# A decoder block in eight-row column tiles: the next block's norm applied 3, 3, 2 instead of 2, 3, 3

## The chip, the cores and the metric

The kernel runs on one core of a Trainium2 chip. The metric is the device time of one execution in microseconds (us). Three executions of the kernel before took 1915.47, 1916.68 and 1917.81 us; the median is 1916.68 us.

## The reference, cut to what matters

One layer, sequence 2048, model width 1024, all float32:

```
h    = rmsnorm(x, norm1)                      # over the 1024 channels
proj = h @ w_in                               # q, k, v, B, C, hc, p: 1792 columns
attn, conv, pool = three mixers on proj       # window-128 attention, conv of 3, trailing means
x    = x + concat(attn, conv, pool) @ w_out   # the output projection
x    = x + relu(rmsnorm(x, norm2) @ w1)^2 @ w2
out  = rmsnorm(x, final_norm)
```

The change concerns the first line of it alone: when the normed rows `h` of the next block of tokens are made.

## The kernel before, in words

Activations are kept transposed: channels on the 128 partitions, tokens on the free axis. The 1024 channels are KC = 8 row tiles, and the sequence is NB = 4 blocks of T = 512 tokens. For each block b the kernel runs the input projection (14 column tiles, from L874 on; each is 8 row tiles times 3 matmuls), the mixers beside it, and then the output projection `out_proj(b, c)` (L736), 8 column tiles c of 24 matmuls each. After the last block come the two MLP matrix products in a Strassen-like form, which the change does not touch.

Every float32 matrix product is made of three matmuls on split operands, high and low part (`mm3`, L284 to L287): high by high (L285), high weight by low data (L286), low weight by high data (L287). So each row tile of the normed input has a high part `xh` and a low part `xl`, and the projection reads the row tiles in the order k = 0 to 7.

`norm_apply(b, k)` (L402) makes one such row tile for a block after the first, with three instructions: VectorE (DVE) multiplies the raw row tile `xr` by the norm's weight and by the broadcast row of reciprocal norms `rb` (`hf`, L417); ScalarE (ACT) casts that to the high part (`xh`, L418); VectorE subtracts (`xl`, L419). These run while TensorE works on the output projection of the block before: the loop over its column tiles (L926 to L930) gives column tiles 0 and 1 the squares, 2 the reciprocal root, 3 the row's store, 4 the row's broadcast load (`rb`, L362), and 5, 6 and 7 the eight applications. `out_proj(b, c)` then adds the residual on VectorE (`xo`, L745), stores it, squares it on ScalarE (`sr`, L752) and adds the square on GpSimd (POOL, `acc`, L753). `hf`, `sr` and others share one pool of four buffers (tag `tmp`).

The weights stream by themselves: SyncE's queue (SP) loads a raw tile `wr` (L208), ScalarE casts the high part `wh` (L263), GpSimd subtracts the low part `wl` (L264).

The order of the instructions on each engine is not the program's text. A planner simulates the engines and gives each free engine the ready instruction that is earliest in the program; the engines then run these orders as they are, and wait where the chip is later than the plan. So an instruction from later in the program can stand ahead of an earlier one. Two such matter here. On ScalarE the first square of the block after next (`acc<-xr`, L383, from `norm_square`) stands among the casts of `norm_apply`: it reads a raw tile that can be loaded only when `norm_apply` has freed the buffer (tag `xr`, 8 buffers). And in the last block the raw buffers go, one by one, to `first_blocks` (L818, called with k = 0 to 3), which loads parts of the residual for the MLP (`xb`, L824), scales them on VectorE (L830) and subtracts them from each other (L784): the scales of the parts with an odd number use a row that is there early (`rb_acc`), the others one that takes the buffer of `rb` and so is loaded (`rb_rb`, L362) after the last `hf` of the block.

Of the kernel before, what the change touches and what calls it, by code (L numbers as in the profile page):

```python
# [84 lines left out]
def tile_trunk(  # L85
# [226 lines left out]
    def tmp(name):  # L312
        return pB.tile([P, T], F32, tag="tmp", name=name, bufs=4)
# [61 lines left out]
    def norm_load(b, k):  # L375
        t = pA.tile([P, T], F32, tag="xr", name=f"xr{b}_{k}", bufs=KC)
        sp.dma_start(t, xT[k * P : (k + 1) * P, b * T : (b + 1) * T])
        xr[b, k] = t
# [12 lines left out]
    def norm_rstd(b):  # L391
        nr[b] = cst.tile([P, 4], F32, tag="nr", name=f"r1_{b}", bufs=2)
        rstd_of(nacc[b], nr[b], starts(T), ps_tr, "tr", f"n1_{b}")

    def norm_bcast(b):
        rbs[b] = pB.tile([P, T], F32, tag="rb", name=f"rb{b}")
        if b == 0:
            act.copy(rbs[b], bcast(nr[b], T, ps_tr, "tr", f"n1_{b}"))
        else:
            row_load(rbs[b], "n1", b * T)  # L400
# [32 lines left out]
    def build_bias():  # L433

        for h in range(NH):
            ps = ps_tr.tile([P, T], F32, tag="tr", name=f"pse{h}")
            pe.matmul(ps[:, :ELEN], rl[:, h : h + 1].to_broadcast([P, P]), oh, start=True, stop=True)

            e = tmp(f"e{h}")[:, :ELEN]
            act.activation(e, ps[:, :ELEN], AF.Copy, scale=math.sqrt(HD))  # L440
            sp.dma_start(esc[h], e)

    def skew_bias():
        full = esc[:]
        skew = bass.AP(full.tensor, full.offset + P - 1, [[ELEN - 1, P], [P * ELEN, NH], [1, 2 * P]])
        sp.dma_start(bias, skew)
# [28 lines left out]
    def load_pw():  # L475
        for g in range(4):
            o = (g % 2) * 64
            sp.dma_start(pwr[o : o + 64, g // 2, o : o + 64], pw[g])
# [3 lines left out]
    def load_rows():  # L482
        for i in range(2):
            for a in range(2):
                rowt[i, a] = pA.tile([P, T], F32, tag="xr", name=f"wr{i}_{a}", bufs=KC)
                sp.dma_start(
                    rowt[i, a].rearrange("p (c n) -> p c n", n=P),
                    wout.rearrange("c p r -> p c r")[:, a * HC : (a + 1) * HC, i * P : (i + 1) * P],
                )

    def build_rows():

        for i in range(2):
            act.activation(pwr[:, i], pwr[:, i], AF.Copy, scale=prm[:, PPS + i : PPS + i + 1])
            t = pA.tile([P, 2 * T], F32, tag="s", name=f"wx{i}", bufs=2)
            for a in range(2):
                ps = ps_tr.tile([P, T], F32, tag="tr", name=f"pwx{i}_{a}")
                pe.matmul(ps, pwr[:, i], rowt[i, a], start=True, stop=True)
                act.copy(t[:, a * T : (a + 1) * T], ps)
            late.append(  # L500
                lambda i=i, t=t: sp.dma_start(wx[:, :, i * P : (i + 1) * P], t.rearrange("p (c n) -> p c n", n=P))
            )
# [16 lines left out]
    def start_first(tiles):  # L519

        ws = [(w_next(0), w_next(0)) for _ in tiles]
        xh, xl = xhl[0]
        pss = [ps_mm.tile([P, T], F32, tag="mm", name=f"pj0_{i}") for i in tiles]
        for step in range(KC + 2 * len(tiles) - 2):
            for n, (w, ps) in enumerate(zip(ws, pss)):
                k = step - 2 * n
                if 0 <= k < KC:
                    hi, lo = w[k // HC]
                    mm3(ps, hi[:, k % HC], lo[:, k % HC], xh[:, k], xl[:, k], k == 0, k == KC - 1)
        first.update(zip(tiles, pss))  # L530

    def proj(b, i, mid=None, bank=None):
        if b == 0 and i in first:
            ps = first[i]
            flush()
        else:
            xh, xl = xhl[b]
            ps = ps_mm.tile([P, T], F32, tag="mm", name=f"pj{b}_{i}") if bank is None else bank
            for k in range(KC):
                if k % HC == 0:  # L540
                    hi, lo = w_next()
                if k == HC and mid:
                    mid()
                latest[0] = mm3(ps, hi[:, k % HC], lo[:, k % HC], xh[:, k], xl[:, k], k == 0, k == KC - 1)
        return ps

    def scaled(b, i, ps):
        if b:
            return ps
        z = pB.tile([P, T], F32, tag="xo", name=f"z{i}", bufs=2)  # L550
        dve.tensor_tensor(out=z, in0=ps, in1=rbs[0], op=ALU.mult)
        return z
# [208 lines left out]
    def norm2_rstd(b, psp, tag):  # L761
        rstd_of(acc2[b], rstd2[:, 4 * b : 4 * b + 4], starts(T), psp, tag, f"n2_{b}")

    def norm2_row(b, psp, tag, t):
        row_store(rstd2[:, 4 * b : 4 * b + 4], "n2", b * T, T, psp, tag, f"n2_{b}", t)
# [96 lines left out]
    for b in range(NB):  # L862
        if b == 0:
            start_first(IN_ORDER[:3])
            load_pw()
            norm_rstd(0)
            build_bias()
            bank = ps_sc.tile([P, 2, T], F32, tag="sc", name="pj0_q")
            first[IN_ORDER[3]] = proj(0, IN_ORDER[3], bank=bank[:, 0])
            norm_bcast(0)  # L870
            skew_bias()
            load_rows()
        for i in IN_ORDER[:NPRE]:
            ps = proj(b, i)  # L874
            evac[i](b, scaled(b, i, ps))
        if b:
            norm2_rstd(b - 1, ps_tr, "tr")
        else:
            build_rows()
        st1, st2 = {}, {}  # L880
        for n, i in enumerate(IN_ORDER[NPRE:]):
            if n < KC and b + 1 < NB:
                norm_load(b + 1, n)

            def mid(n=n):
                if 2 <= n < 10:
                    st2[n] = att_trans(*st1.pop(n - 2))

            ps = proj(b, i, mid)
            if b and n == 1:  # L890
                norm2_row(b - 1, ps_tr, "tr", tmp(f"row2_{b}"))
            if 2 <= n < 10:
                av = att_av(*st2.pop(n))
            evac[i](b, scaled(b, i, ps))
            if 2 <= n < 10:
                att_out(*av, dve if n > 5 else gp)
            if n < 8:
                st1[n] = att_scores(b, *units[n])
            if n == 5:
                do_pool(b, 0)  # L900
            elif n == 7:
                do_pool(b, 1)
            if 2 <= n < 4 and b + 1 < NB:
                norm_square(b + 1, n - 2, gp)
            if b + 1 == NB:
                with tc.issue_after(latest[0].ins):
                    if n == 0:
                        first_rows()
                    for k, at in enumerate(FIRST):
                        for step in range(3):  # L910
                            if n == at[step]:
                                first_blocks(k, step)
        if b + 1 == NB:
            sA.close()
            pH, sH = opened("pH", bufs=1, side="right")
            pX, sX = opened("pX", bufs=1, side="right")
        for c in range(KC):
            if b + 1 < NB:
                if c < 2:
                    for k in range(2 + c * 6 // 2, 2 + (c + 1) * 6 // 2):  # L920
                        norm_square(b + 1, k, dve)
                elif c == 2:
                    norm_rstd(b + 1)
                elif c == 3:
                    row_store(nr[b + 1], "n1", (b + 1) * T, T, ps_tr, "tr", f"n1_{b + 1}", tmp(f"row1_{b}"))
                elif c == 4:  # L926
                    norm_bcast(b + 1)
                else:
                    for k in {5: (0, 1), 6: (2, 3, 4), 7: (5, 6, 7)}[c]:
                        norm_apply(b + 1, k)  # L930
            else:
                per = NEARLY * HC / KC
                if c == 0:
                    for i in range(int(per)):
                        first_load(i)
                for i in range(int(per * c), int(per * (c + 1))):
                    first_take(i)
                for i in range(int(per * (c + 1)), int(per * (c + 2))):
                    if i < NEARLY * HC:
                        first_load(i)  # L940
            out_proj(b, c)
# [400 lines left out]
```

## Time and profile before

| what | value |
|---|---|
| median of three executions | 1916.68 us |
| the profiled execution's own time | 1912.7 us |
| its span on the core | 1910.9 us |
| TensorE (PE) busy | 1875.3 us, 98% of the span |
| VectorE busy | 1114.4 us, 58% |
| ScalarE busy | 894.2 us, 47% |
| GpSimd busy | 1020.9 us, 53% |

The profile is of one execution. The span is what the core's instructions cover, and the profiled execution's time is 1.8 us more. Engines run beside each other; an engine's idle time costs something only where TensorE, which is busy nearly all of the span, has to wait because of it. Below, a row of a timeline gives the start and the length in us, the engine, the line, the operation, what it writes and reads, a count of merged instructions, and in brackets the idle time before it and what ended that. "Boundary" is the passage from one block's output projection to the next block's input projection; there are three.

### The profile page before, as it was taken

To read this page: it belongs to the slowest core of one execution; us is meant where nothing else is said; L and a number is where in the kernel's file an instruction comes from. 1 tells how busy PE (TensorE), PEld (TensorE's weight loads), DVE (VectorE), ACT (ScalarE), POOL (GpSimd) and SP (SyncE) were. 2 spreads that over 40 slices of the span, in tenths; PEclk is the share of its full clock that TensorE was granted. 3 is DMA by queue.
4 is the path that set the end of the run, shared out by engine and by line. 5 is a ranking of instruction groups with operands and counts; after the bars stand their busy time and mean duration, and the time that the engine had idled before them with its cause. 6 is when DMAs were issued, how large, how long until landed. Compare 5 with 4: busy or idle time off the path is not lost.

```text
span 1910.9 us, 25904 instructions
## 1 busy us (share of the span) xinstructions
PE 1875.3 (98%) x8507; PEld 1527.7 (80%) x8507; DVE 1114.4 (58%) x1606; ACT 894.2 (47%) x1637; POOL 1020.9 (53%) x745
## 2 busy tenths in 40 slices
PE   8989999999899999999999999999999999999998
PEld 6867887888787888888878888888888888888887
DVE  5695585576888577865574444442525264533465
ACT  6654664663476444554565455442323222225332
POOL 5667566575563645654464444434666665526520
PEclk9999999999999999999999999999999999999999
DMA  8417426425936779765686656588777666645244
GB/s 261 139 61 219 123 67 208 129 72 183 313 105 217 241 252 316 274 219 195 226 282 202 198 178 194 187 276 281 238 236 237 196 214 203 221 131 166 99 160 138
DMA packets 202938, 375.46 MB, mean 196 GB/s; under 512 B 22775, under 2 KB 43316, under 8 KB 202804
## 3 DMA queue, kind: packets, MB, share of 16 engines
q1 hardware_dynamic: 201992, 373.20, 60.3%
q8 instruction: 67, 1.10, 0.2%
q10 hardware_dynamic: 812, 0.61, 0.1%
q14 instruction: 67, 0.55, 0.1%
HBM read 249.45 MB, written 117.98 MB: 192 GB/s over the span
## 4 chain that ended last, share of the span: by engine, by line
PE 84%; DMA 6%; DVE 6%; issue 2%; ACT 1%; POOL 1%; SPq 1%; DVEq 0%; POOLq 0%; ACTq 0%
PE o L285 11%; PE o L286 11%; PE o L287 11%; PE bT L287 6%; PE bT L286 6%; PE bT L285 6%; PE bB L285 4%; PE bB L286 4%; PE bB L287 4%; PE pj L286 4%; PE pj L285 4%; PE pj L287 4%; PE po L286 1%; PE po L285 1%; PE po L287 1%
## 5 line engine op out<-in xcount | busy, mean ns | idle before, releaser
L264 POOL TENSOR_TENSOR wl<-wr,wh 128x512 fp32r<-128x512 f32 x354 | 502.9, 1427 | 516.0 <-ACT wh L263 477.8
L263 ACT CAST wh<-wr 128x512 fp32r<-128x512 f32 x416 | 254.5, 617 | 345.5 <-PE bT L286 62.6
L784 DVE TENSOR_TENSOR bl<-br,bh 128x1024 fp32r<-128x1024 f32 (+2 forms) x144 | 186.9, 1301 | 320.9 <-ACT bh L1131 318.0
L286 PE MATMUL o<-bl,wh 128*128 128x512 f32 (+1 forms) x960 | 362.0, 380 | 0.0
L287 PE MATMUL o<-bh,wl 128*128 128x512 f32 (+1 forms) x960 | 361.2, 380 | 0.0
L285 PE MATMUL o<-bh,wh 128*128 128x512 f32 (+1 forms) x960 | 349.7, 380 | 0.0
L286 PEld LDWEIGHTS o<-bl,wh 128*128 128x128 f32 x960 | 180.9, 188 | 36.6 <-DVE bl L784 0.2
L287 PEld LDWEIGHTS o<-bh,wl 128*128 128x128 f32 x960 | 180.8, 188 | 36.7
L285 PEld LDWEIGHTS o<-bh,wh 128*128 128x128 f32 x960 | 176.4, 188 | 36.4
L286 PE MATMUL bT<-hlT,wh 128*128 128x512 f32 x512 | 202.2, 395 | 1.0 <-POOL hlT L987 1.0
L287 PE MATMUL bT<-hhT,wl 128*128 128x512 f32 x512 | 202.0, 395 | 0.0
L285 PE MATMUL bT<-hhT,wh 128*128 128x512 f32 x512 | 201.8, 394 | 0.0
L285 PE MATMUL pj<-xh,wh 128*128 128x512 f32 x440 | 177.7, 405 | 7.0 <-ACT wh L263 6.5
L286 PE MATMUL pj<-xl,wh 128*128 128x512 f32 x440 | 176.2, 401 | 4.1 <-DVE xl L419 4.1
L287 PE MATMUL pj<-xh,wl 128*128 128x512 f32 x440 | 176.3, 401 | 0.0
L264 POOL TENSOR_TENSOR wl<-s,wh 128x512 fp32r<-128x512 f32 x64 | 92.2, 1440 | 137.7 <-ACT wh L263 128.9
L263 ACT CAST wh<-s 128x512 fp32r<-128x512 f32 x64 | 39.7, 621 | 247.4 <-PE o L286 238.8
L1131 ACT CAST bh<-br 128x1024 fp32r<-128x1024 f32 (+2 forms) x144 | 123.2, 856 | 64.4 <-PE o L287 55.5
L285 PE MATMUL bB<-hhB,wh 128*128 128x512 f32 x384 | 151.7, 395 | 0.0
L286 PE MATMUL bB<-hlB,wh 128*128 128x512 f32 x384 | 151.4, 394 | 0.0
L287 PE MATMUL bB<-hhB,wl 128*128 128x512 f32 x384 | 151.3, 394 | 0.0
L231 POOL TENSOR_TENSOR s<-wr,wr 128x512 f32<-128x512 f32 x64 | 127.9, 1999 | 15.3 <-DMA wr<-in_w_dram 10.6
(186 smaller groups left out, 3368.5 us busy)
## 6 DMA issues: line engine op xcount, KB each, us to landing
wr<-in_w_dram SPq DMA_DIRECT2D x256, 256.0 KB, 3.6
hop_T<-s SPq DMA_DIRECT2D x128, 256.0 KB, 2.9
wr<-in_win_dram SPq DMA_DIRECT2D x112, 256.0 KB, 4.3
hop_B<-h SPq DMA_DIRECT2D x96, 256.0 KB, 3.3
br<-hop_B SPq DMA_DIRECT2D x48, 512.0 KB, 4.5
br<-hop_T SPq DMA_DIRECT2D x48, 512.0 KB, 4.5
wr<-ss_T SPq DMA_DIRECT2D x48, 256.0 KB, 2.9
wr<-in_wout_dram SPq DMA_DIRECT2D x36, 256.0 KB, 2.6
```

What stands on the lines that cost most here:

```text
L231: gp.tensor_tensor(out=t, in0=a, in1=b, op=op)
L263: act.copy(hi, src)
L264: eng.tensor_tensor(out=lo, in0=src, in1=f32(hi), op=ALU.subtract)
L285: pe.matmul(ps, hi, xh, start=first, stop=False)
L286: pe.matmul(ps, hi, xl, start=False, stop=False)
L287: return pe.matmul(ps, lo, xh, start=False, stop=last)
L784: return dve.tensor_tensor(out=out, in0=a, in1=b, op=ALU.subtract)
L1131: mark["act"] = act.copy(hi, src)
```

## The change

In the loop over the output projection's column tiles, the eight applications of the next block's norm are dealt out differently: column tile 5 gets row tiles 0, 1 and 2 instead of 0 and 1, column tile 6 gets 3, 4 and 5 instead of 2, 3 and 4, and column tile 7 gets 6 and 7 instead of 5, 6 and 7. Nothing else is edited.

```
@@ -926,7 +926,7 @@
                 elif c == 4:
                     norm_bcast(b + 1)
                 else:
-                    for k in {5: (0, 1), 6: (2, 3, 4), 7: (5, 6, 7)}[c]:
+                    for k in {5: (0, 1, 2), 6: (3, 4, 5), 7: (6, 7)}[c]:
                         norm_apply(b + 1, k)
             else:
                 per = NEARLY * HC / KC
```

## Rows read from the trace of the kernel before

**Rows 1.** Waits of TensorE over the whole span: total us, times, longest us.

```profile
PE pj L286 <- DVE xl L419: 4.1, 4, 2.9
...
PE sc L610 <- DMA q<-ql: 3.4, 5, 1.5
```

**Rows 2.** Timeline of TensorE at the first boundary.

```profile
182.51 0.39 PE L285 MATMUL pj<-xh,wh 128*128 128x512 f32 x1
...
183.81 0.39 PE L285 MATMUL pj<-xh,wh 128*128 128x512 f32 x1
```

**Rows 3.** Timeline of TensorE at the second boundary.

```profile
329.46 0.39 PE L285 MATMUL pj<-xh,wh 128*128 128x512 f32 x1
...
332.94 0.40 PE L285 MATMUL pj<-xh,wh 128*128 128x512 f32 x1
```

**Rows 4.** Timeline of TensorE at the third boundary, into the last block.

```profile
474.54 0.40 PE L285 MATMUL pj<-xh,wh 128*128 128x512 f32 x1
...
477.81 0.39 PE L287 MATMUL pj<-xh,wl 128*128 128x512 f32 x1
478.73 0.50 PE L285 MATMUL pj<-xh,wh 128*128 128x512 f32 x1 [0.53 <-ACT xh L418]
482.10 0.80 PE L286 MATMUL pj<-xl,wh 128*128 128x512 f32 x1 [2.87 <-DVE xl L419]
...
488.63 0.40 PE L285 MATMUL pj<-xh,wh 128*128 128x512 f32 x1
```

**Rows 5.** One stretch there: busy us by engine, granted TensorE clock, DMA share, GB/s.

```profile
484.00:486.00 2.00, 2.00 (x5) 1.59 (x6) 2.00 (x4) 0.32 (x1) 0.00 (x0) 0.50 0.89 289
```

**Rows 6.** Timeline of VectorE at the second boundary, column tiles 5 to 7.

```profile
313.84 1.35 DVE L419 TENSOR_TENSOR xl<-hf,xh 128x512 fp32r<-128x512 f32 x2
316.93 0.69 DVE L745 TENSOR_TENSOR xo<-po,xo 128x512 f32<-128x512 f32 x1 [1.74 <-DMA xo<-in_xT_dram]
...
325.25 0.68 DVE L745 TENSOR_TENSOR xo<-po,xo 128x512 f32<-128x512 f32 x1
325.85 3.55 DVE L417 SCALAR_TENSOR_TENSOR hf<-xr,prm,rb 128x512 f32<-128x512 f32 x3
329.33 2.98 DVE L419 TENSOR_TENSOR xl<-hf,xh 128x512 fp32r<-128x512 f32 x3
```

**Rows 7.** Timeline of ScalarE in the same stretch.

```profile
318.85 0.63 ACT L383 ACTIVATE acc<-xr 128x512 f32<-128x512 f32 x1 [3.86 <-DMA xr<-in_xT_dram]
```

**Rows 8.** Timeline of VectorE at the third boundary.

```profile
461.84 1.46 DVE L419 TENSOR_TENSOR xl<-hf,xh 128x512 fp32r<-128x512 f32 x2
467.69 0.75 DVE L830 SCALAR_TENSOR_TENSOR xb<-xb,prm,rb_acc 128x512 f32<-128x512 f32 x1 [4.40 <-DMA xb<-x1s]
468.36 0.69 DVE L745 TENSOR_TENSOR xo<-po,xo 128x512 f32<-128x512 f32 x1
...
477.28 3.08 DVE L417 SCALAR_TENSOR_TENSOR hf<-xr,prm,rb 128x512 f32<-128x512 f32 x3
480.29 4.03 DVE L419 TENSOR_TENSOR xl<-hf,xh 128x512 fp32r<-128x512 f32 x3
...
485.50 4.80 DVE L830 SCALAR_TENSOR_TENSOR xb<-xb,prm,rb_rb 128x512 f32<-128x512 f32 x4
```

**Rows 9.** The instructions of tile hf: ns min/median/max, first and last start, forms.

```profile
L417 DVE SCALAR_TENSOR_TENSOR hf<-xr,prm,rb x24: 737/745/1793, 163.1 to 478.6; 128x512 f32<-128x512 f32 x24
...
L419 DVE TENSOR_TENSOR xl<-hf,xh x24: 676/770/1791, 165.2 to 483.6; 128x512 fp32r<-128x512 f32 x24
```

**Rows 10.** Timeline of the SyncE queue at the third boundary.

```profile
480.39 0.32 SPq L362 DMA_DIRECT2D rb_rb<-row_n  x1
```

**Rows 11.** Timelines of VectorE and TensorE in the last block's input projection.

```profile
499.78 0.68 DVE L594 TENSOR_TENSOR ql<-pj,q 64x512 fp32r<-64x512 f32 x1
...
509.27 0.36 PE L610 MATMUL sc<-Kd,q 128*128 128x256 f32 x1 [1.55 <-DMA q<-ql]
509.59 0.39 PE L285 MATMUL pj<-xh,wh 128*128 128x512 f32 x1
```

More of the change, by code (lines that the diff above doesn't have):

```diff
@@ L928, in tile_trunk @@
                 else:
-                    for k in {5: (0, 1), 6: (2, 3, 4), 7: (5, 6, 7)}[c]:
+                    for k in {5: (0, 1, 2), 6: (3, 4, 5), 7: (6, 7)}[c]:
                         norm_apply(b + 1, k)
```

## The prediction

> **What bounds the kernel now.** I read first the waits of TensorE, then its timeline at the three boundaries, then the timelines of the engines that make it wait there. TensorE is the bound nearly everywhere, so only what makes it wait counts. Among its waits the reader is to see that matmuls on the low part of the normed input (`xl`) waited 4 times, 4.1 us in all and 2.9 at the longest [rows 1]. All four lie at the three boundaries, where the next block's input projection begins and the last applications of the norm are not done.
>
> The wait alone is not the price. At full clock one matmul follows another every 0.234 us: 15 matmuls of row tiles 0 to 4 start from 474.54 to 477.81, 14 steps [rows 4]. First boundary: three steps from 182.51 to 183.81 took 1.30 us in place of 0.70, so 0.60 is lost [rows 2]. Second: nine steps from 329.46 to 332.94 took 3.48 in place of 2.10, 1.38 lost [rows 3]. Third: sixteen steps from 477.81 to 488.63 took 10.82 in place of 3.74, 7.08 lost [rows 4]. There TensorE stood still for 0.53 and 2.87 us and then had a granted clock of 0.50, the 1.2 GHz level [rows 5]: the 14 steps from 482.10 to 488.63 took 6.53 in place of 3.27, so 3.26 of the loss is the clock. All three boundaries together hold 9.06 us, 0.5% of the time; that is the most this change can fetch where it acts.
>
> Why VectorE is late: in column tiles 6 and 7 it has six instructions of `norm_apply` and one residual add. At the second boundary the last six run from 325.85 to 332.31, 6.46 us or 1.08 each [rows 6]; at the third from 477.28 to 484.32, 7.04 or 1.17 each [rows 8]. Seven of these are more than TensorE's 24 x 0.234 = 5.6 us for a column tile. In column tile 5 it has four, and then stands idle: 1.74 us before `xo` at 316.93, which waited for its own load [rows 6], and 4.40 us before 467.69, where a scale of `first_blocks`, planned ahead of `xo`, waited for a transfer [rows 8].
>
> **The change part by part.** It adds, removes and resizes no instruction. Six groups of three (`hf`, `xh`, `xl`) move: row tiles 2 and 5 at three boundaries, each one column tile earlier. No DMA is issued by them; but the buffer that `hf` reads comes free earlier, so one load of a raw tile (or of `xb`) on SyncE's queue may go earlier. That I cost at nothing: these loads are wanted a block later, and the queue's other loads have five weight tiles of lead over TensorE. If the cover is gone, it is a load ahead of the weights on that queue, 0.3 to 0.4 us of issue (0.32 for one such [rows 10]).
>
> Column tile 5: `hf` and `xl` of row tile 2 on VectorE cost from 0.737 + 0.676 = 1.41 to 1.793 + 1.791 = 3.58 us [rows 9]; by the mean of 1.08, 2.16. The idle 1.74 takes nearly all of it [rows 6]; 0.4 is left over, and `xo` comes that much later. Queued behind `xo` are its store, its square and the next group's `hf`. The next group's first `xl` stood idle anyway for a cast behind the square at 318.85, which itself waited 3.86 us for a load [rows 7], so the 0.4 is swallowed there. I take nothing for it; its bounds are 0 and 3.58 - 1.74 = 1.84.
>
> Column tile 6 has as many instructions as before, others by number. I leave `xo` at 325.25 [rows 6].
>
> Column tile 7 has four in place of six. Second boundary: 325.85 + 4 x 1.08 = 330.2 for the last `xl` instead of 332.31. TensorE wants it seven steps after 329.46, at 331.1. The loss of 1.38 goes, with 0.9 to spare. First boundary: the last `xl` was late by 0.60 and comes 2.16 earlier. The loss goes. Together 1.98 us, from 0.60 (the second stays) to 1.98.
>
> Third boundary: in column tile 5 the scale at 467.69 still waits for its transfer, which began when the second `hf` freed a buffer, and that is not moved. The new pair fits into the 4.40 us of standing idle, and `xo` stays at 468.36 [rows 8]. Column tile 7 then runs from 477.28 to 477.28 + 4 x 1.17 = 482.0 in place of 484.3: VectorE is 2.34 us ahead. TensorE wants row tile 6 at 474.54 + 19 x 0.234 = 479.0 and 7 at 479.7, gets them at 480.8 and 482.0, and so still loses about 2.3, and up to 3.3 more if its clock falls again. It gains between 1.5 and 4.8 there.
>
> What is late next: in the last block VectorE's queue is full behind this. It goes straight on to the scales at 485.50 [rows 8] and, with the subtractions and evacuations between, to `ql` at 499.78; the first score matmul at 509.27 waits 1.55 us for the DMA of that `ql` [rows 11]. So whatever TensorE gains beyond VectorE's 2.34 it gives back at that wait. I take 2.2 for the third boundary, between 0 (the transfers of `first_blocks` hold the chain) and 7.08.
>
> Sum: 1.98 + 2.2 = 4.2 us. Against the profiled execution's own time, 1912.7 us (1910.9 of span and 1.8 around it), that is 1908.5. This execution is 4.0 below the median of the runs shown, 1916.68, from which the same 4.2 gives **1912.5 us**.
>
> One rule speaks against this sum. The row first: the 24 `hf` have a median of 745 ns and a maximum of 1793 [rows 9], so an instruction is either plain or held up. The Trainium skill (SBUF — State Buffer, SBUF: two separate sides) says that VectorE with two SBUF inputs and GpSimd reading SBUF share a port pair by an exclusive lock, held for a whole instruction. The trace agrees in the two kinds of duration. By that rule the delay belongs to GpSimd's instructions, whose number does not change, and a pair taken out saves only its plain time.
>
> **The rivals.**
> The pair is cheap: GpSimd's work delays what is left in column tile 7 as often as before, and the pair saves 1.41 instead of 2.34 at the third boundary. The second still fits (332.31 - 1.41 = 330.9 against 331.1). Gain 1.98 + 1.4 = 3.4, 1913.3 us. For it: the two kinds of duration [rows 9]. Against: six instructions and three of GpSimd don't meet in a fixed way.
>
> The last block is held by its transfers: the row for the later scales (`rb_rb`) is loaded at 480.39, after the last `hf` [rows 10], and the queue, stores and loads behind it may not come earlier when VectorE does. Then the third boundary's gain ends as a longer wait at 509.27, and 1.98 is left: 1914.7 us. For it: the DMA share of 0.89 [rows 5]. Against: the load is issued as soon as `hf` has gone, and that is earlier.
>
> The planner puts `xo` ahead of the scale, since VectorE comes free later in its plan too. Then the rest of the idle, 4.40 - 2.34, and the scale itself (468.36 - 467.69) leave the path as well: 2.34 + 2.06 + 0.67 = 5.1, in all 7.1, 1909.6 us. Against: the scale was planned before `xo` with 4.4 us of room on the chip, and 1.4 to 2.3 of it are used.
>
> Slower: at the first two boundaries the cast of row tile 2 is planned behind the square that waits until 318.85 [rows 7]. Now that `xl` of row tile 2 stands ahead of `xo`, `xo` waits too: square done at 319.5, cast and subtraction 1.3 more, `xo` at 320.8, six instructions of 1.08 from 321.5 to 328.0, four more after the next `xo` from 328.7 to 333.0, against 331.1 wanted. The loss at the second boundary becomes 1.9 + 0.1, that of the first grows alike, 0.6 each, so the 1.98 turns into -1.2, and the third leaves +2.2. What decides is the clock: it stayed up after a stall of 1.55 (the next matmul took 0.39 [rows 11]) and fell after 0.53 and 2.87 [rows 4, 5]. One fall costs 3.26: -2.2 + 1.2 + 3.3 = +2.3, 1919.0 us; without it 1915.7. For it: the square does stand among these casts. Against: it needs a transfer that begins when the first `hf` is done, and the new cast needs only the third.
>
> **How the numbers follow.** My forecast has 0.42, the cheap pair 0.13, held by transfers 0.18, `xo` ahead 0.14, slower 0.13. The likeliest is 1912.5, by itself 1911.0 to 1914.0. The range of 1909.0 to 1918.0 takes in nearly all but the fall of the clock and the far half of `xo` ahead. About 0.2%, 3.8 us, is what a measurement of this kernel can tell from no change; the forecast lies just past it. Faster by more: some two thirds of the forecast, `xo` ahead, a little of the cheap pair, 0.45. Within: the rest of these, held by transfers, and the slower case without a fall, 0.45. Slower by more: 0.10.
>
> **What would show it.** After the change TensorE should have no wait for `xl` at the first two boundaries; at the third the last `xl` should end near 482.0 less the 2 us gained before, `xo` of column tile 5 should still stand behind the waiting scale, and the wait of the scores for `ql` should be longer than 1.55. I am wrong if the first two waits stay, if the square stands ahead of the third cast, if VectorE is no earlier after the third boundary, or if TensorE's waits are gone and the time is the same.

## The result and the profile after

The changed kernel takes 1919.04 us (median of 20 runs, 1913.21 to 1923.42), the kernel before 1915.03 (20 runs, 1911.16 to 1917.81): a ratio of 1.0021, 95% interval 1.0013 to 1.0029. It is slower by about 4 us; 4.2 faster was forecast. The profiled execution has a span of 1913.5 us and an own time of 1915.3, so it is one of the quicker ones. Executions of one kernel lie up to 12 us apart (1908.1 to 1920.4 in one kernel below), so below the ratios decide, and a trace only shows where its own execution went.

The waits of TensorE over the whole span, after (total us, times, longest):

```profile
PE sc L610 <- DMA q<-ql: 6.6, 6, 4.1
...
PE pj L286 <- DVE xl L419: 3.3, 2, 2.6
...
PE sc L610 <- ACT vt L575: 1.2, 1, 1.2
```

Against [rows 1] the waits for `xl` fall from 4.1 to 3.3 us, and both that are left are at the third boundary. The waits of the scores for the query copies (`q<-ql`) double, from 3.4 to 6.6, and one for `vt` is new. TensorE's timeline at the second boundary, which shows no wait for `xl` any more, and behind it the first score matmuls (`sc`) of the block that begins there. That is block 2, counted from 0; the expectations below call it block 1:

```profile
350.94 0.36 PE L610 MATMUL sc<-Kd,q 128*128 128x256 f32 x1 [1.24 <-ACT vt L575]
...
352.47 0.36 PE L610 MATMUL sc<-Kd,q 128*128 128x256 f32 x1 [1.05 <-DMA q<-ql]
...
353.40 0.63 PE L287 MATMUL pj<-xh,wl 128*128 128x512 f32 x1
```

The profile puts the first wait down to `vt`, a copy on ScalarE that ended at 350.78. But the scores do not need it: before, the first of them ran ahead of that copy. Before, TensorE and ScalarE:

```profile
350.35 0.28 PE L610 MATMUL sc<-Kd,q 128*128 128x256 f32 x1
```

```profile
351.00 0.59 ACT L575 COPY vt<-pj 128x512 f32<-128x512 f32 x1
```

The first query copy, issued at 343.62, took 7.2 us to land, until 350.85, so the first wait too is one for the copies. Windows over the same place (us, busy us by engine, granted clock, DMA share, GB/s):

```profile
352.00:354.00 2.00, 1.53 (x6) 0.94 (x6) 0.00 (x0) 0.00 (x0) 0.00 (x0) 0.76 1.04 271
354.00:356.00 2.00, 2.00 (x7) 1.71 (x7) 0.00 (x0) 0.00 (x0) 0.00 (x0) 0.50 0.80 206
```

Behind the two waits the clock is at the 1.2 GHz level for a while (0.50). From the first matmul of the input projection to the first transpose of the softmax (`pt`, L638), the stretch in which all this lies, the second boundary took 36.50 us before and takes 39.32 after, although the 1.38 of [rows 3] is gone. The first took 36.29 and takes 36.37: most of its 0.60 of [rows 2] went into waits for `q` (0.4 before, 0.6 after) and for a weight cast (0.3).

Why are the copies late? They are issued on SyncE's queue, which starts its DMAs one after the other and waits at the head for what the next one needs. The queue before, at the second boundary (start, us, operation):

```profile
324.35 0.33 SPq L743 DMA_DIRECT2D xo<-in_xT_dram  x1
324.77 0.38 SPq L377 DMA_DIRECT2D xr<-in_xT_dram  x1
...
325.96 0.33 SPq L746 DMA_DIRECT2D x1s<-xo  x1
327.06 0.33 SPq L377 DMA_DIRECT2D xr<-in_xT_dram  x1
...
330.52 0.33 SPq L743 DMA_DIRECT2D xo<-in_xT_dram  x1
...
337.11 0.33 SPq L743 DMA_DIRECT2D xo<-in_xT_dram  x1
...
338.00 0.63 SPq L566 DMA_DIRECT2D Kd<-Kd  x1
...
340.83 0.99 SPq L598 DMA_DIRECT2D q<-ql  x1
```

and after:

```profile
326.56 0.33 SPq L743 DMA_DIRECT2D xo<-in_xT_dram  x1
326.98 0.38 SPq L377 DMA_DIRECT2D xr<-in_xT_dram  x1
327.45 0.38 SPq L208 DMA_DIRECT2D wr<-in_win_dram  x1
327.93 0.38 SPq L746 DMA_DIRECT2D x1s<-xo  x1
328.36 0.86 SPq L377 DMA_DIRECT2D xr<-in_xT_dram  x1
...
334.46 0.33 SPq L743 DMA_DIRECT2D xo<-in_xT_dram  x1
...
339.98 0.33 SPq L743 DMA_DIRECT2D xo<-in_xT_dram  x1
...
340.87 0.63 SPq L566 DMA_DIRECT2D Kd<-Kd  x1
...
343.62 0.49 SPq L598 DMA_DIRECT2D q<-ql  x1
```

The loads of the raw tiles (`xr`) of the block after next, whose buffers come free earlier, have moved up by one: between the residual load and the store of column tile 6 (`x1s`) stood the fifth of them before (324.77) and stands the sixth after (326.98), and three in place of two are ahead of the store of column tile 5. The store of column tile 6 is issued 1.97 us later (TensorE itself is 0.39 later). The load of a residual tile (`xo`, two buffers) waits for that store: it is issued 4.56 us behind it before, 6.53 after, with three raw loads in between before and two after. The next `xo` load waits in the same way for the store of column tile 7, and right behind it come the key copies: they start 12.0 us after the projection before, 14.5 after, and the first query copy slips by 2.8 (0.39 of it TensorE's).

The two loads that hold the queue there are not urgent themselves. They are the 17th and 18th of the 32 `xo` loads, eight to a block, so they are for column tiles 0 and 1 of block 2; VectorE's add that reads the first of them runs at 439.06 before, 108 us after its issue. To hold these two behind the copies was not tried.

VectorE there, after, in column tiles 5 to 7:

```profile
317.68 0.69 DVE L745 TENSOR_TENSOR xo<-po,xo 128x512 f32<-128x512 f32 x1 [0.71 <-DMA xo<-in_xT_dram]
...
326.22 0.68 DVE L745 TENSOR_TENSOR xo<-po,xo 128x512 f32<-128x512 f32 x1
...
329.63 1.46 DVE L419 TENSOR_TENSOR xl<-hf,xh 128x512 fp32r<-128x512 f32 x2
```

Against [rows 6] the work of the norm ends earlier, at 331.09 for the last `xl` in place of 332.31, but the residual add of column tile 6 comes 0.97 later.

The third boundary. VectorE, after:

```profile
470.49 0.75 DVE L830 SCALAR_TENSOR_TENSOR xb<-xb,prm,rb_acc 128x512 f32<-128x512 f32 x1 [1.82 <-DMA xb<-x1s]
471.16 0.68 DVE L745 TENSOR_TENSOR xo<-po,xo 128x512 f32<-128x512 f32 x1
...
480.07 1.40 DVE L417 SCALAR_TENSOR_TENSOR hf<-xr,prm,rb 128x512 f32<-128x512 f32 x2
481.40 1.78 DVE L830 SCALAR_TENSOR_TENSOR xb<-xb,prm,rb_acc 128x512 f32<-128x512 f32 x1
483.10 3.44 DVE L419 TENSOR_TENSOR xl<-hf,xh 128x512 fp32r<-128x512 f32 x2
```

The idle time before the waiting scale shrinks from 4.40 [rows 8] to 1.82, as forecast. But in column tile 7 a scale of 1.78 us has come ahead of the last two `xl`. The last one ends 8.8 us after TensorE started this projection, against 9.8 before: 1.0 earlier, not the 2.34 of the prediction. TensorE there, after:

```profile
484.90 0.50 PE L286 MATMUL pj<-xl,wh 128*128 128x512 f32 x1 [2.59 <-DVE xl L419]
...
486.59 0.80 PE L286 MATMUL pj<-xl,wh 128*128 128x512 f32 x1 [0.73 <-DVE xl L419]
...
512.02 0.55 PE L610 MATMUL sc<-Kd,q 128*128 128x256 f32 x1 [4.09 <-DMA q<-ql]
```

The eleven steps from 481.92 to 489.68 took 7.76 us in place of 2.57: the loss is 5.19, where it was 7.08 [rows 4]. The 1.9 us gained, and more, come back as the wait of 4.09, where it was 1.55 [rows 11]: the first score matmul runs 34.3 us after the projection's start, against 34.7 before. The clock behind it is at 0.50, where it had stayed at 1.00.

### The profile page after: what moved, and what is told of

Its sections match the earlier page's. It is cut to its first block, busy times and chain, and to the rows that moved or that the text cites. A ratio compares the mean times of both kernels' runs of the same rounds, so it can differ in the third digit from the quotient of the medians.

```text
span 1913.5 us, 25908 instructions
## 1 busy us (share of the span) xinstructions
PE 1875.4 (98%) x8507; PEld 1528.4 (80%) x8507; DVE 1118.4 (58%) x1606; ACT 893.0 (47%) x1637; POOL 1023.0 (53%) x745
## 4 chain that ended last, share of the span: by engine, by line
PE 85%; DMA 6%; DVE 5%; issue 1%; ACT 1%; POOL 1%; SPq 1%; DVEq 0%; POOLq 0%; ACTq 0%
PE o L286 11%; PE o L285 11%; PE o L287 11%; PE bT L287 6%; PE bT L286 6%; PE bT L285 6%; PE bB L286 4%; PE bB L285 4%; PE bB L287 4%; PE pj L286 4%; PE pj L285 4%; PE pj L287 4%; PE po L286 2%; PE po L285 2%; PE po L287 2%
```

## The experiments

All ratios are to the kernel before, with 95% intervals. "Boundary 1" and "2" are the stretch named above (first `pj` to first `pt`), "last" the stretch from the first `pj` of the last block to the row statistics near 665 us, each from row starts of TensorE's timeline in one profiled execution. With no wait above 0.3 us in it, boundary 1 or 2 takes 34.5 to 35.0. One execution says little: three kernels with the old order and no held loads have the same work up to 470 us and took 36.50, 36.95 and 40.77 at boundary 2; three with the new order 39.32, 38.07 and 36.95. The copies come late in some executions of the old order too, and the two boundaries together differ by only 1.1 us in the mean of these three and three (74.2 and 75.3). That the changed order loses there is told by the ratios; the traces tell how. Their waits separate the kernels better than their lengths. Waits of the first scores for the copies in both stretches together (those put down to `vt` counted in):

- new order, raw loads early, two residual buffers (changed kernel, boundaries 1 and 2 only, scales held, square moved): 2.9, 3.6, 3.2, 4.7 us;
- old order, raw loads not held (before, boundary 3 only, scales held, square moved): 0.6, 1.6, 1.4, 2.2 us;
- either order, raw loads held behind the copies (eight kernels): 0 to 1.1 us;
- the new order with three residual buffers 1.8, with the raw loads behind the last store 5.3; the old order with nine raw buffers 2.3 us.

Every edit is planned anew as a whole, so two kernels differ in more places than the edited line. In the edits, `issue_after` keeps an instruction from being planned ahead of the one named.

```
kernel                                     ratio (interval)         b. 1   b. 2   last
before (2, 3, 3)                           1                        36.29  36.50  192.32
changed (3, 3, 2)                          1.0021 (1.0013, 1.0029)  36.37  39.32  191.47
3,3,2 at boundaries 1 and 2 only           1.0022 (1.0008, 1.0036)  37.46  38.07  193.17
3,3,2 at boundary 3 only                   1.0008 (0.9996, 1.0020)  37.11  36.95  192.42
3,3,2, raw loads behind query copies       0.9991 (0.9977, 1.0006)  34.88  35.85  193.27
2,3,3, raw loads behind query copies       0.9993 (0.9983, 1.0003)  36.31  37.45  190.53
3,3,2, raw loads behind the last store     1.0039 (1.0024, 1.0055)  40.83  39.47  193.79
3,3,2, raw tiles 1-7 behind the copies     0.9990 (0.9979, 1.0001)  34.74  36.09  194.00
3,3,2, square behind the last cast         1.0032 (1.0022, 1.0042)  39.55  39.43  193.19
2,3,3, square behind the last cast         1.0004 (0.9992, 1.0017)  37.12  36.00  190.58
3,3,2, three residual buffers              1.0014 (1.0002, 1.0026)  39.01  36.21  194.38
2,3,3, nine raw buffers                    0.9992 (0.9982, 1.0002)  36.23  36.96  187.22
3,3,2 at 1 and 2, raw loads held           0.9981 (0.9969, 0.9993)  34.56  34.86  193.16
3,3,2, raw loads and scales held           0.9968 (0.9956, 0.9981)  34.53  36.58  185.24
2,3,3, raw loads and scales held           0.9981 (0.9967, 0.9995)  35.79  38.93  190.68
3,3,2, scales held                         1.0013 (1.0003, 1.0024)  37.67  36.95  188.62
2,3,3, scales held                         0.9981 (0.9969, 0.9993)  34.96  40.77  189.35
3,3,2, raw loads and residual loads held   1.0000 (0.9989, 1.0011)  34.88  34.89  190.87
3,3,2, all three held                      0.9984 (0.9975, 0.9994)  34.88  34.88  192.03
```

**Which boundary.**

```diff
-for k in {5: (0, 1, 2), 6: (3, 4, 5), 7: (6, 7)}[c]:
+for k in ({5: (0, 1, 2), 6: (3, 4, 5), 7: (6, 7)} if b + 2 < NB else {5: (0, 1), 6: (2, 3, 4), 7: (5, 6, 7)})[c]:
```

In the second kernel the two orders change places.

> The new order 3, 3, 2 at the first two boundaries only; the third boundary keeps 2, 3, 3. My theory (queue order): the raw tiles that come free one column tile earlier at the second boundary put their loads ahead of a store and a load of the residual on SyncE's queue, the query copies of block 1 come 2 to 3 us later, and the scores wait for them. Then this kernel has no wait for xl at 182 and 329 us, but waits of about 1 us each for vt and q at 350 to 353 us with a fallen clock behind them, and is 2.5 to 4 us slower than before. Rival (the third boundary is the cause, where a scale was planned ahead of the last two xl): then this kernel has the gain of the first two boundaries alone, about 2 us faster than before.

> The new order 3, 3, 2 at the third boundary only. My theory (queue order at the second boundary): nothing changes up to 474 us, and the third boundary and the last block together give back what they lose: 0 to 1 us faster than before. Rival (the third boundary is the cause: the scale ahead of the last two xl, the scores of the last block waiting 4.1 us for q with the clock down behind them): 3 to 4 us slower than before.

The first two boundaries alone lose as much as the whole change. The third alone is not told from no change, and its stretch shows no gain; its interval goes from 0.8 us gained to 3.8 lost.

**Raw loads held behind the query copies, in both orders.**

```diff
-late.append(lambda o=o, z=z, a=a: sp.dma_start(f32(q[z : z + 64, a]), ql[o : o + 64]))
+late.append(lambda o=o, z=z, a=a: last_q.__setitem__(i, sp.dma_start(f32(q[z : z + 64, a]), ql[o : o + 64])))
...
-if n < KC and b + 1 < NB:
-    norm_load(b + 1, n)
+if 0 < n <= KC and b + 1 < NB:
+    with tc.issue_after(last_q[1].ins) if b else ExitStack(): norm_load(b + 1, n - 1)
```

> The changed kernel, with the loads of the raw tiles of the block after next held back on SyncE's queue until the second query copies of block 1 are issued (they are wanted a block later). My theory (queue order): the waits for vt and q at 350 to 353 us go, the clock stays up there, and the time is 3 to 4.5 us below the changed kernel, 0 to 2 below the kernel before. Rival (third boundary): no difference from the changed kernel. Rival (the transfers as such are what delays the copies, wherever they stand in the queue): a gain here too, and none when the loads stand just ahead of the copies.

> The kernel before with the same hold on the loads of the raw tiles. My theory: in the kernel before these loads already stood behind the store and the load that matter, so only about 0.2 us of waits for q at 350 to 352 us can go: the same as before within 1 us. If holding these loads is worth as much here as in the changed kernel (3 us or more), the hold is an improvement of its own and does not show that the changed order was the cause.

The hold takes 6 us from the changed kernel (1912.64) and under 2 from the kernel before, within its noise. In the changed kernel with the hold both boundaries come to within 1 us of the stretch without waits.

**Only behind the last store.** The same hold, on the store of column tile 7 in place of the query copy.

> The changed kernel with the loads of the raw tiles held on SyncE's queue only until the last store of the residual (column tile 7) is issued. They then stand behind every load and store of the residual of that boundary, but ahead of or among the key and query copies. If position behind the store and the residual's loads is what counts, the key copies at the second boundary are issued by 339 us again, the waits at 350 us go, and the time is within 1.5 us of the kernel that holds them until the query copies (1912.6). If it is the loads' transfers that delay the copies, these eight transfers now fall right on the copies: the waits for q stay or grow, and the time is that of the changed kernel (1919) or above.

It has the worst ratio of all. SyncE's queue at the second boundary of this kernel:

```profile
335.75 0.87 SPq L746 DMA_DIRECT2D x1s<-xo  x1
336.68 0.97 SPq L377 DMA_DIRECT2D xr<-in_xT_dram  x2
...
338.16 2.60 SPq L377 DMA_DIRECT2D xr<-in_xT_dram  x4
...
341.40 2.24 SPq L377 DMA_DIRECT2D xr<-in_xT_dram  x2
343.96 0.33 SPq L743 DMA_DIRECT2D xo<-in_xT_dram  x1
344.68 0.63 SPq L566 DMA_DIRECT2D Kd<-Kd  x1
```

The eight loads are behind the store, but another load of the residual and the key copies are behind them. My first reading, that the store is what they must not pass, was too narrow: they must not pass the copies. Whether issue or transfer costs more here isn't separated.

**The square or the loads.** The hold had moved a second thing. In the changed kernel, as in [rows 7], the square of raw tile 0 stands on ScalarE ahead of the casts of column tile 6 and waits 3.63 us for its load; with the loads held it is gone from there. Two edits move one each:

```diff
+# the square alone
-act.copy(xh[:, k], hf)
+last_xl[0] = act.copy(xh[:, k], hf)
...
+with tc.issue_after(last_xl[0].ins) if b else ExitStack(): norm_square(b + 1, n - 2, gp)
```

```diff
+# raw tiles 1 to 7 alone; tile 0 is loaded as before
+with tc.issue_after(last_q[1].ins) if b and n > 1 else ExitStack():
+    [norm_load(b + 1, k) for k in ([0] if n == 0 else [n - 1] if n > 1 else [])]
```

> The changed kernel with only the square of the first raw tile of the block after next held on ScalarE behind the last cast of xh; the raw loads stay early on SyncE's queue. In the changed kernel this square waits 3.6 us for its load and three casts stand behind it. Theory A (the early raw loads on SyncE's queue): the residual add of column tile 6 comes 1 to 2 us earlier, but the loads still stand ahead of its store and of the load of column tile 7: key and query copies late, 1916 to 1919. Theory B (the square ahead of the casts is what makes VectorE and then the store late; the hold on the loads helped because it moved the square away): as the hold on all loads, 1911 to 1914, key copies of block 1 less than 13 us after the projection starts.

> The changed kernel with raw tiles 1 to 7 held on SyncE's queue until the query copies, but raw tile 0 loaded as before, so that its square stands ahead of the casts as in the changed kernel. Theory A (SyncE's queue): the gain of the hold on all eight, 1911 to 1914. Theory B (the square): 1917 to 1920, VectorE waiting 1.5 us for xh in column tile 6 and the scores at 350 us waiting for q.

> The kernel before with the same hold on the square alone. Theory A: within 1.5 us of before, since its last xl, not the copies, are what comes late. Theory B: 1 to 4 us faster than before, as in the changed kernel, because the square delays column tile 6 here too.

This decides for the loads (0.9990 against 1.0032). With them held and the square left where it was, VectorE and ScalarE are as late as in the changed kernel:

```profile
317.07 0.64 ACT L383 ACTIVATE acc<-xr 128x512 f32<-128x512 f32 x1 [3.35 <-DMA xr<-in_xT_dram]
```

```profile
319.29 4.25 DVE L419 TENSOR_TENSOR xl<-hf,xh 128x512 fp32r<-128x512 f32 x3 [1.51 <-ACT xh L418]
```

and yet the copies on SyncE's queue are early (the projection starts at 323.49, so the first key copy is 10.9 us behind it), and the scores at 346 us wait 0.7 in all:

```profile
324.18 0.33 SPq L746 DMA_DIRECT2D x1s<-xo  x1
...
326.72 0.33 SPq L743 DMA_DIRECT2D xo<-in_xT_dram  x1
...
334.40 0.63 SPq L566 DMA_DIRECT2D Kd<-Kd  x1
```

With the square moved and the loads early (projection at 330.79) the first key copy is 14.5 behind, as in the changed kernel, and the scores wait:

```profile
345.30 0.63 SPq L566 DMA_DIRECT2D Kd<-Kd  x1
```

```profile
355.55 0.36 PE L610 MATMUL sc<-Kd,q 128*128 128x256 f32 x1 [1.38 <-ACT vt L575]
357.08 0.42 PE L610 MATMUL sc<-Kd,q 128*128 128x256 f32 x1 [1.06 <-DMA q<-ql]
```

**The wait at the head of the queue.** Three buffers for the residual tile: `bufs=2` becomes `bufs=3` at the tag `xo`.

> The changed kernel with three buffers for the residual tile in place of two, so that its load on SyncE's queue no longer waits for the store of the tile two before; the raw loads stay early. Theory (the raw loads delay a store and lengthen its transfer, the residual's load waits for that store at the head of the queue, and the key and query copies stand behind it): the key copies of block 1 are issued less than 13 us after the projection starts in place of 14.5, the waits at 350 us shrink to under 0.6 us, and the time falls to 1913 to 1916. Rival (the early raw loads cost by their own transfers and issue): key copies and waits stay as in the changed kernel, 1918 to 1920.

At the second boundary the theory holds: the first key copy is at 337.51, 11.7 us after the projection's start at 325.80, and the stretch is 36.21. The total is no better: the first boundary takes 39.01 in this execution, and a third buffer reorders the queue from block 0 on. So one trace agrees with the place, and the time does not confirm it.

**Early loads without the moved norm.** `bufs=KC` becomes `bufs=KC + 1` at the tag `xr`, in the kernel before.

> The kernel before, its order of the norm (2, 3, 3) untouched, with nine buffers for the raw tiles in place of eight: each raw load then waits for one application of the norm less, and at the second boundary stands on SyncE's queue where it stands in the changed kernel (raw tile 4 ahead of the residual load of column tile 7, raw tile 5 ahead of the store of column tile 6). Theory (the early raw loads are the cause): the store of column tile 6 and all behind it slip by 2 us, the scores at 350 us wait 1.5 us or more in all, and this kernel is slower than before by 1 to 4 us although the norm was not moved. Rival (the cause lies in the moved norm instructions themselves, on VectorE, ScalarE or GpSimd): the same as before within 1 us.

No loss, against the theory as put. But its trace shows an exchange. Neither of the first two boundaries has a wait for `xl` any more (1.2 us in the kernel before), although the order is the old one; in their place the scores wait 2.3 us for the copies (0.6 before), and the two stretches are together 73.2, no shorter than 72.8. The old order with the square moved shows the same: no wait for `xl`, 2.2 us for the copies, 73.1. So in these traces the copies are what is late next, whatever makes `xl` early.

The first key copy is 12.5 us behind the projection here, not 14.5, although the raw loads stand as in the changed kernel: the square is no longer among the casts, only two row tiles lie in column tile 5, and the residual add of column tile 6 comes at 322.36, 2.9 us ahead of the projection (0.1 ahead after the change). The last block, which shares these buffers, is shorter as well (187.22). So early loads alone are not shown to make the time longer; they go with the larger loss where the store they pass is late already, as it is with three row tiles ahead of it. That last step is read from the traces, not tried by itself.

**The order alone.** The new order at boundaries 1 and 2, the old at 3, raw loads held.

> The new order at the first two boundaries, the old at the third, raw loads held until the query copies. Beside the kernel before with the same hold (1913.2, 0.07% below before) it shows what the forecast's first two boundaries are worth by themselves. Theory: 2 to 4 us less, 1909.5 to 1911.5, with no wait for xl or q above 0.5 us at either boundary. Rival (the hold gives all there is): 1913.

At 1911.63 it lies 0.12% under the old order with the same hold, inside the intervals, but its two stretches are 69.4 us in place of 73.8: no wait for `xl` or `q` is left in them.

**The third boundary.** Scales of `first_blocks` held on VectorE behind the last `xl`; loads of its later parts (`xb`) held on SyncE's queue behind the query copies:

```diff
-with tc.issue_after(latest[0].ins):
+with tc.issue_after(latest[0].ins), tc.issue_after(last_xl[0].ins):       # scales
-first_blocks(k, step)
+with tc.issue_after(last_q[1].ins) if k > 1 and step == 0 else ExitStack(): first_blocks(k, step)
```

> The kernel with the raw loads held until the query copies, and the scales of the last block held on VectorE until the last xl is issued, so that none stands ahead of the last two xl. The last xl then ends about 1.8 us earlier against the start of the projection and TensorE's wait for xl at the third boundary shrinks from 3.1 to under 1.5 us; if that is a gain, the time falls by up to 2 us plus the clock's part, to about 1910. My theory says that TensorE then only waits longer for q at the first scores (5 us and more): within 1 us of 1912.6, or slower, since the scales and what they free come later.

> The kernel with the raw loads held until the query copies, and in the last block the later loads of the residual (xb) held until then too. At the third boundary three of these loads stand ahead of the first query copy in the new order, one in the old. My theory (the same queue, a second time): the first two query copies are issued 1.2 us apart as in the old order instead of 3.1, the scores of the last block wait 1.5 us or less in place of 3.7, the clock does not fall there, and the third boundary with the last block gains 1.5 to 3 us: about 1910.5. Rival (VectorE sets it: ql itself is late): the wait stays at 3 us or more and the time at 1912.6; and holding the loads may make the norm of the last block late, plus 1 to 3 us.

> All three holds together. If the third boundary is held by the two things one after the other (the scale ahead of the last xl, then the loads ahead of the query copies), only this one collects both: 2 to 4 us below 1912.6, the score wait of the last block under 2.5 us. If the scales' delay makes the last block's norm late, the gain is eaten at the output projection of the last block (waits for xo at 600 to 625 us grow beyond 2.1 us): no better than 1912.6.

My theory missed. With the scales held the time falls to 1908.0, the fastest of all: 0.32% below before. VectorE in that kernel (TensorE's projection starts at 472.58):

```profile
470.44 0.68 DVE L745 TENSOR_TENSOR xo<-po,xo 128x512 f32<-128x512 f32 x1
471.04 1.84 DVE L417 SCALAR_TENSOR_TENSOR hf<-xr,prm,rb 128x512 f32<-128x512 f32 x2
472.91 3.38 DVE L419 TENSOR_TENSOR xl<-hf,xh 128x512 fp32r<-128x512 f32 x2
476.21 4.14 DVE L830 SCALAR_TENSOR_TENSOR xb<-xb,prm,rb_acc 128x512 f32<-128x512 f32 x3
...
494.10 0.68 DVE L594 TENSOR_TENSOR ql<-pj,q 64x512 fp32r<-64x512 f32 x1
```

The last `xl` ends 3.7 us after the start (9.8 before, 8.8 after the change), and `ql` comes 21.5 us after it (25.2 before, 24.0 after): VectorE no longer stands waiting for an `xb` ahead of the residual add, and this lead reaches the scores. TensorE now waits 3.0 us for VectorE's `Kd` on the way, but its wait for `q` is 0.6, and the first score matmul runs 30.4 us after the projection's start (34.7 before). Holding the `xb` loads brings the first two query copies to 1.3 us apart in place of 3.1 and the wait from 3.7 to 2.1, but the statistics of the last block's scores are then waited for (2.2 us on `nm`), and the ratio does not move. The three together (0.9984) are worse than the two without it.

> The kernel before (2, 3, 3) with both holds: raw loads until the query copies, scales of the last block behind its last xl. With the same holds the order 3, 3, 2 stands at 1908.0 (0.32% below before). If the order 3, 3, 2 is worth what was forecast once nothing takes it back, this one keeps the waits for xl at the three boundaries and stands 2 to 4 us above, at 1910 to 1912. If the holds alone make the gain, it stands at 1908 as well, and the order of the norm is worth nothing.

> The kernel before with the scales held alone. If the scale that waits for its transfer ahead of the residual add of column tile 5 (4.4 us of VectorE standing idle at the third boundary) is on the path, this is 2 to 5 us faster than before, with the last xl of the third boundary 4 us earlier. If the last block only waits for its query copies, it is within 1 us of before.

> The changed kernel with the scales held alone; raw loads as in the changed kernel. The second boundary should lose as in the changed kernel (waits for vt and q of about 1 us each at 350 us, 2 to 4 us lost), the third should gain as with both holds: 1919 less 4 to 6, so 1913 to 1915, level with before. If it comes to 1908, the second boundary was not a cause.

In the old order holding the scales gives 0.19%, and 0.12% beside the hold on the loads; in the new order 0.23% beside it, and 0.08% without: there the loss of boundaries 1 and 2 stays, as expected. Between 0.9968 and 0.9981, the two orders with both holds, the intervals overlap: that 3, 3, 2 by itself is faster by 0.1% is likely, not shown.

## Why the prediction was wrong

**What failed** is what the prediction says of DMA in the change: "No DMA is issued by them; but the buffer that `hf` reads comes free earlier, so one load of a raw tile (or of `xb`) on SyncE's queue may go earlier. That I cost at nothing". I had the mechanism and looked only at who wants these loads (a block later) and at the weights' lead. I did not list what stands behind them on the queue: the store of the residual, the load that waits for it, and the key and query copies, whose lead over the first scores is nil: a wait of 0.2 to 0.4 us stood there before. The price I set, 0.3 to 0.4 us of issue, came out as 2.5 us for the copies, and with two waits and a lowered clock as 2.8 us of boundary 2 after a gain of 1.38 there. With these loads held behind the copies the changed kernel takes 0.9991 of the time before in place of 1.0021; the same hold in the old order gives 0.9993. What stays open is how they cost it. With nine raw buffers they stand as early in the old order and the time is no longer, so by themselves they are not shown to be enough; and their place in the queue, their issue and their transfers were not told apart.

**The first two boundaries:** the norm's own steps were right. VectorE takes the pair in the idle time of column tile 5 (`xo` at 317.68, where 0.71 of idle is left; 0.4 later was forecast, 0.36 came beyond TensorE's own 0.39). The last `xl` ends at 331.09, less the 0.39 that is 330.7, where 330.2 was forecast. TensorE waits for no `xl`. The 1.98 was there to be had: in the six kernels with the new order there and the loads held, the two stretches together are 1.7 to 3.4 us shorter than in the kernel before (72.79 together). "Late next" was asked for the last block only, and not here. The sliding of 0.4 us "swallowed" in column tile 6 was not swallowed: the residual add there came 0.97 later, 0.58 beyond TensorE's offset.

**The third boundary:** forecast +2.2, of which the trace shows 1.9 at TensorE's `xl` and 0.4 at the first scores; the kernel with the new order there alone shows no gain (1.0008). The step "column tile 7 then runs ... 4 x 1.17" left out that the place of the scales is planned anew: 1.78 us of scale came ahead of the last two subtractions. "Whatever TensorE gains beyond VectorE's 2.34 it gives back at that wait" was right in kind: 1.55 became 4.09. The rival with `xo` ahead of the scale did not happen, but the kernel with the scales held is that rival made true, and its last stretch is 7.1 us shorter than before, where 5.1 was worked out; by the medians of the two kernels with the loads held the scales are worth 4.6.

**The rival for slower** gave 1919.0, the time that came, by another road: the square ahead of the new cast. The new cast stands ahead of the square, and moving the square did not help (1.0032), so that this number came out is luck. Its clock term was right in kind: the clock fell at 353, behind 2.3 us of waits. The 3.26 us that it gives a fall are some 0.5 too many: three of the 14 steps (from 482.10, 483.12 and 483.77) took 0.59 to 0.65 us, the others 0.43. **By the rule on the shared port** the pair would save only plain time: the 48 `hf` and `xl` add up to 50.1 us before and 52.7 after, and over all kernels here to 46.9 to 53.9 without a split by order, so their total did not fall with the regrouping; who holds them up is not tried here.

**The range** ended at 1918.0, one us below the result, and slower had a chance of 0.10, because I looked for slow mechanisms on VectorE, ScalarE and the clock, and not on SyncE's queue.

## What to carry to other kernels

When an edit frees a buffer earlier, find the load that waits for it, and read what stands behind that load on its in-order queue, down to the next consumer without slack; a load wanted a block later goes behind the copies wanted now (here the raw tiles; for the two residual loads right ahead of the copies it was not tried). Ask "what is late next" at each place where time is gained, not at the largest alone, and hold planned work in place before an order is judged: here two holds give 0.19% in the old order, and the new order beside them another 0.13%, which is within the noise. A gain of VectorE in front of TensorE counts only as far as the next transfer that TensorE waits for comes earlier too.

## What the hardware showed

The store of column tile 6 kept the load that waits for it back by 4.56 us before, 6.53 after, and by 2.54 and 4.57 in two kernels with raw loads held, where only weights stand around it. So the early loads may lengthen it, but it varies by 2 us without them. The Trainium skill (DMA: Bandwidth & Descriptors, Issuing engines are not separate DMA queues) says that DMAs from all issuing engines interleave on the same 16 DMA engines, and that issuing from several saves only the issue time, usually small beside the transfer. The issue time here is indeed small, 0.3 to 1.0 us for a raw load that then takes 4.9 to 6.1 us to land, as far as the trace tells. The longer times stand at the head of the queue: the residual loads held SyncE's queue up for 6.0 us between 320 and 346 us before and for 10.6 after, and what stood behind them came later. The length of the standstill alone does not tell the cost: it is 9.5 us with all raw loads held, and there the copies come early. A second queue for the raw loads was not tried.
